# Experts' matrices laid out pair by pair, and one gate piece of each pair loaded for both experts into a tile of twice the size

## The chip, the cores and the metric

The kernel runs on one core of one Trainium2 chip. The metric is device time in microseconds of one execution. The core's five engines are called PE (TensorE, matrix multiplication), DVE (VectorE), ACT (ScalarE), POOL (GpSimd) and SP (SyncE, which here only issues DMAs). A row of the profile's page or of the trace calls them by these names; a DMA issued from SP stands there as SPq.

## The reference

A trunk of two layers over 512 tokens of width 1024, all in float32. A layer is attention in three parallel groups of heads (neighbourhood attention on a grid, latent attention "MLA", windowed attention with a sink) and then a layer of 16 experts in which each expert chooses its tokens:

```python
DEPTH, SEQ, D_MODEL, N_EXPERTS, EC_CAPACITY, D_EXPERT = 2, 512, 1024, 16, 2, 1024
# per layer:
#   h = h + W_out . concat_g( RMSNorm_g( mixer_g(split_g(RMSNorm(h) @ W_in)) ) )
#   h = h + ExpertChoiceSwiGLU(RMSNorm(h))
# ExpertChoiceSwiGLU: each expert takes its SEQ * EC_CAPACITY / N_EXPERTS = 64 best tokens x_e and adds
#   gain * ( (silu(x_e @ w_gate[e]) * (x_e @ w_up[e])) @ w_down[e] )   to their rows
```

Each expert has three matrices of 1024 x 1024 (gate, up, down), 4 MB each, so that a layer's experts are 192 MB, and both layers' 384 MB; every one of these bytes is read once.

## The kernel before, in words

**The expert stage.** Two experts, e and e + 1, make a pair; 64 tokens of each stand side by side on PE. A layer has eight pairs, here called pair 0 to pair 7. The matrices of a pair are read in 24 pieces of 1 MB, each a tile of 128 partitions x 2048 numbers: 8 of gate, 8 of up, 8 of down, always one for e and one for e + 1 behind it. `weights` loads gate pieces (two blocks of 128 rows each), `col_half` up and down pieces; pair 0's first gate pieces are read in halves of 512 KB by `both`. `expert_mm` multiplies; its order is pinned to that of the code. A piece of both experts is 16 matmul instructions on PE (rows call them `in<-ew` or `S<-ew`, line 1163).

**The buffers.** Nearly every large tile of the program, in attention too, comes from one pool, `big`, of 25 buffers of 1 MB (8 KB in each partition): the experts' pieces (`ew`), the input projections' raw matrices (`wraw`), their high and low parts, the up-projection of MLA (`uraw`, split into `uh` and `ul`), the bias tiles of neighbourhood attention (`nab`, 896 KB, one for each of its two pairs of heads and loaded in line 871), the output projection (`woraw`). A tile takes a buffer when the last reader of the tile that had it before is done.

**What sets the order.** The program is written as units that are merged by hand and then put into each engine's order by a scheduler that works before the run; the order of SP's DMAs and the buffer that each tile takes are fixed by it. SP issues its DMAs strictly in that order: one that waits for a buffer holds up all behind it. Each DMA also waits for the DMA eight places ahead of it (eight semaphores, named DMAHW0 to DMAHW7 in the rows of the order), so that eight at most are in flight. The experts' loads of a layer start during its attention, when buffers come free, and then run to the layer's end.

**Names.** "NA pair 2" is the second pair of heads of neighbourhood attention; its scores are the matmuls `S<-nak,naq` (line 856), to which DVE adds the second `nab` tile in line 861. The MLA up-projection multiplies with `uh` and `ul` in lines 161 to 163.

Of the kernel before, what the change touches and what calls it, by code (L numbers as in the profile page):

```python
# [9 lines left out]
F32 = mybir.dt.float32  # L10
# [6 lines left out]
P = 128  # L17
D = 1024
S = 512
NT = S // P  # L20
KD = D // P
DEPTH = 2
NEXP = 16
# [27 lines left out]
C_PERM = C_TRI + 128  # L51
NCST = C_PERM + 512

NB_B = 25
PR = {'SWA': 0, 'NA': 0, 'MLA': 0, 'up': 0}
WARM = [30, 0, 0, 0]
PSB = [2, 1, 1]
# [4 lines left out]
def build(tc, x, w_in, w_uq, w_ukv, w_out, w_gate, w_up, w_down, pv, wr, cst, nab, fin, out):  # L62
    nc = tc.nc
    ctx = ExitStack()
    with ctx:
        const = ctx.enter_context(tc.tile_pool(name="const", bufs=1))
        bpool = ctx.enter_context(tc.tile_pool(name="big", bufs=NB_B))
        spool = ctx.enter_context(tc.tile_pool(name="sm", bufs=1))
        tiny = ctx.enter_context(tc.tile_pool(name="tiny", bufs=2))
        ps = ctx.enter_context(tc.tile_pool(name="ps", bufs=1, space=bass.MemoryType.PSUM))  # L70
# [3 lines left out]
        def nm(s):  # L74
            cnt[0] += 1
            return f"{s}_{cnt[0]}"

        def big(s, dt=F32):
            return bpool.tile([P, 2048], dt, name=nm(s), tag="b")

# [10 lines left out]
        def recut(n):  # L93
            cut[:] = [big("cut", F32R if i == 0 else F32) for i in range(n)]
# [132 lines left out]
        if globals().get("_POOLS") is not None:  # L227
            _POOLS.extend([const, bpool, spool, tiny])

        h = [big("h").rearrange("p (t d) -> p t d", t=NT) for _ in range(2)]  # L230
        c = const.tile([P, NRES], F32, name="c")
        pvt = const.tile([P, DEPTH, NPV], F32, name="pvt")
# [89 lines left out]
        def open_layer(L):  # L322
# [3 lines left out]
            def load(j):  # L326
                raw = big("wraw")[:, :1536].rearrange("p (k n) -> p k n", n=384)
                nc.sync.dma_start(raw, w_in[L, j * 512:(j + 1) * 512, 1184:1568].rearrange("(k p) n -> p k n", p=P))
                w[j] = raw, *(big(n, F32R)[:, :1536].rearrange("p (k n) -> p k n", n=384) for n in ("wh", "wl"))
# [32 lines left out]
        for L in range(DEPTH):  # L362
# [727 lines left out]
            for u in range(NT - 1):  # L1090
                n = NT - 1 - u
# [11 lines left out]
            nc.vector.tensor_tensor(ps2, pcv, ge, op=ALU.mult)  # L1103
            nc.vector.tensor_tensor(pos, ps2[:, :, 0], ps2[:, :, 1], op=ALU.add)

            def weights(w_, e, k0, n):

                ws = []
                for a in range(2):
                    wt = big("ew").rearrange("p (k n) -> p k n", k=n)  # L1110
                    nc.sync.dma_start(wt, w_[L, e + a, k0 // n].rearrange("p (k n) -> p k n", k=n))
                    ws.append(wt)
                return k0, n, ws

            def both(w_, e, k):

                wt = big("ew").rearrange("p (a k n) -> p a k n", a=2, k=1)
                for a in range(2):
                    nc.sync.dma_start(wt[:, a, 0], w_[L, e + a, k // 2, :, k % 2 * D:(k % 2 + 1) * D])
                return k, 1, [wt[:, 0], wt[:, 1]]  # L1120

            def col_half(w_, e, n, ms, cs=slice(0, 512)):

                pieces, k0 = [], 0
                for m in ms:
                    ws = []
                    for a in range(2):
                        wt = big("ew")[:, :m * (cs.stop - cs.start)].rearrange("p (k n) -> p k n", k=m)
                        if cs.stop - cs.start < 512:
                            src = w_[L, e + a, n, cs.start // 256].rearrange("p (k n) -> p k n", k=KD)  # L1130
                            nc.sync.dma_start(wt, src[:, k0:k0 + m])
                        else:
                            src = w_[L, e + a, n, k0 // 4].rearrange("p (k n) -> p k n", k=4)
                            nc.sync.dma_start(wt, src[:, k0 % 4:k0 % 4 + m])
                        ws.append(wt)
                    pieces.append((k0, m, ws))
                    k0 += m
                return pieces

            def up_half(e, n):  # L1140
                return col_half(w_up, e, n, (4, 4))

            def down_half(e, n, ms=(4, 4), cs=slice(0, 512)):
                return col_half(w_down, e, n, ms, cs)

            gate0 = [both(w_gate, 0, k) for k in range(KN["b1"])]
            gate0 += [weights(w_gate, 0, k, 2) for k in range(KN["b1"], KD, 2)]
            up0 = [up_half(0, n) for n in range(2)]
            down0 = [down_half(0, n) for n in range(2)]
# [70 lines left out]
            def hidden(e, gate_w=(), up_w=(), ahead=None, before=None, then=None):  # L1220
# [50 lines left out]
                for i in range(n_gate):  # L1271
                    piece = gate_w[i] if gate_w else weights(w_gate, e, i * 2, 2)
                    k = piece[0] + piece[1]
                    gather_to(k)
                    if done < len(steps):
                        gather_to(k0s[done] + 1)
                    expert_mm(og, xs, piece)
                    if i == i_places:
                        if before:
                            before()  # L1280
                        places()
                    if i == n_gate // 2 and then:
                        then()
# [85 lines left out]
            for e in range(0, NEXP - 2 * tail, 2):  # L1369
                then = None  # L1370
                if e == 4:
                    def then():
                        held.pop(0)()()
                p = hidden(e, gate_w, up0 if e == 0 else (), before=rest, then=then)
                down_w = down0 if e == 0 else [down_half(e, n) for n in range(2)]
                gate_w = [weights(w_gate, 2, k, 2) for k in range(0, KD, 2)] if e == 0 else ()
                if e == 0:
                    held += [half_then(n, down_w[n], *p, held=True) for n in range(2)]
                    continue
                if e == 2:  # L1380
                    token_parts(0)
                rest = half_then(0, down_w[0], *p, held.pop(0)() if e == 4 else None)
                if e == 2:
                    token_parts(1)
                rest = half_then(1, down_w[1], *p, rest)
                if e == 2:
                    st["gather"]()
# [3 lines left out]
            for e in range(NEXP - 2 * tail, NEXP, 2):  # L1391
# [6 lines left out]
                if e < NEXP - 2:  # L1398
                    p = hidden(e, gate_w, (), ahead, rest)
                    gate_w = nxt["gate"]  # L1400
                else:
                    p = hidden(e, gate_w, before=rest)
# [125 lines left out]


def _pairs(w):  # L1530
    return w.reshape(DEPTH, NEXP, 4, 2, P, D).transpose(0, 1, 2, 4, 3, 5).reshape(DEPTH, NEXP, 4, P, 2 * D)


def _halves(w):
    return (w.reshape(DEPTH, NEXP, 2, 4, P, 2, 512).transpose(0, 1, 5, 2, 4, 3, 6)
             .reshape(DEPTH, NEXP, 2, 2, P, 2048))


def _last_quarters(w):

    w = np.array(w)
    v = w[-1, -2:, 1].reshape(2, 2, P, 4, 2, 256)
    w[-1, -2:, 1] = v.transpose(0, 4, 2, 1, 3, 5).reshape(2, 2, P, 2048)
    return w


def _arrays(inp):
    inp = {k: np.asarray(v) for k, v in inp.items()}
    return {
        "x": inp["x"].reshape(S, D),  # L1550
        "w_in": inp["w_in"],
        "w_uq": inp["mla_w_uq"],
        "w_ukv": inp["mla_w_ukv"],
        "w_out": inp["w_out"],

        "w_gate": _pairs(inp["w_gate"]),
        "w_up": _halves(inp["w_up"]),
        "w_down": _last_quarters(_halves(inp["w_down"])),
        "pv": _pack(inp),
        "wr": inp["w_router"].reshape(DEPTH, KD, P, NEXP).transpose(0, 2, 1, 3).reshape(DEPTH, P, NWR),  # L1560
        "cst": _constants(),
        "nab": _na_bias(inp["na_rpb"]),
        "fin": np.ascontiguousarray(np.broadcast_to(inp["final_norm"][None], (P, D))),
    }
# [17 lines left out]
```

## Time and profile before

| | |
|---|---|
| three timed runs | 1532.13, 1536.1, 1537.83 us; median 1536.1 |
| profiled execution | 1538.31 us, of which the span of the trace is 1535.2 us |
| clock granted to PE, mean | 0.985 |
| PE busy | 1454.9 us (95% of the span) |
| DMA | 444.98 MB, mean 290 GB/s over the span |

The time of the profiled execution holds 3.1 us that lie outside the span; it is 2.2 us above the median of the timed runs. All times below count from the span's start. In layer 0 the attention goes on to about 305 us and the experts to about 752; in layer 1 the attention ends at about 1072 and the experts at about 1520.

### The profile page before, as it was taken

What the parts mean: (1) busy time and instruction counts of PE and PEld (TensorE: products, weight loads), DVE (VectorE), ACT (ScalarE), POOL (GpSimd) and SP (SyncE); (2) the same over time, 40 slices, a digit from 0 to 9 for tenths busy, and PEclk for the clock granted to TensorE, in tenths of its full rate; (3) what the DMA queues carried; (4) which work ended last, traced back from release to release, by engine and by line L of the source; (5) the groups of instructions that cost most, each with busy time, mean ns of one, the idle gap of its engine ahead of it and who ended that gap; (6) DMA issues with size and microseconds to landing.
All of it is one profiled execution on the core that took longest, in us unless ns stands there. A gap on an engine that the chain in (4) does not pass through costs nothing.

```text
span 1535.2 us, 21197 instructions
## 1 busy us (share of the span) xinstructions
PE 1454.9 (95%) x8262; PEld 861.9 (56%) x8262; DVE 597.6 (39%) x1513; ACT 364.7 (24%) x939; POOL 241.0 (16%) x341
## 2 busy tenths in 40 slices
PE   9999999899999999987999998898999999999886
PEld 8987877544444434432489876675444344344323
DVE  6766675710222212110376587557102222121113
ACT  4434645300200000001134355442001000000012
POOL 3532442000200000000133335320002000000002
PEclk9999999999999999999999999999999999999998
DMA  5122263789999999999711214447899999999996
GB/s 201 51 71 78 83 190 142 310 332 397 390 415 421 421 420 421 421 421 418 304 55 53 69 51 141 132 157 306 329 397 394 415 421 421 421 421 421 421 421 243
DMA packets 80434, 444.98 MB, mean 290 GB/s; under 512 B 7760, under 2 KB 23632, under 8 KB 32464
## 3 DMA queue, kind: packets, MB, share of 16 engines
q1 hardware_dynamic: 76688, 438.40, 71.5%
q0 software_dynamic: 3648, 5.24, 1.7%
q8 instruction: 65, 1.06, 0.3%
q14 instruction: 33, 0.27, 0.1%
HBM read 436.28 MB, written 2.10 MB: 286 GB/s over the span
## 4 chain that ended last, share of the span: by engine, by line
PE 78%; DMA 14%; DVE 4%; ACT 2%; issue 1%; POOL 1%; DVEq 0%; SPq 0%; ACTq 0%; POOLq 0%
PE S L1163 20%; PE in L1163 15%; PE in L161 5%; DMA ew<-in_w_up_dram 5%; PE in L163 5%; PE in L162 5%; PE tr L155 4%; PE o L297 4%; DMA ew<-in_w_down_dram 4%; DMA ew<-in_w_gate_dram 4%; PE tr L1213 3%; PE tr L1200 2%; PE tr L1341 2%; PE trq L1341 1%; DMA mq<-mq 1%; PE trq L998 1%
## 5 line engine op out<-in xcount | busy, mean ns | idle before, releaser
L1163 PE MATMUL S<-ew,PT 128*64 128x512 f32 x960 | 214.0, 595 | 2.4 <-DMA ew<-in_w_down_dram 2.4
L1163 PE MATMUL S<-ew,xs 128*64 128x512 f32 x768 | 173.6, 594 | 11.8 <-DMA ew<-in_w_up_dram 11.8
L1163 PE MATMUL in<-ew,xs 128*64 128x512 f32 x768 | 172.6, 595 | 5.6 <-DMA ew<-in_w_gate_dram 5.6
L1163 PEld LDWEIGHTS S<-ew,PT 128*64 128x64 f32 x960 | 67.0, 137 | 133.2 <-issue 127.3
L1298 DVE SCALAR_TENSOR_TENSOR sb<-S,rsl,sb 128x512 f32<-128x512 f32 x32 | 24.0, 751 | 302.5 <-PE S L1163 302.5
L1163 PEld LDWEIGHTS S<-ew,xs 128*64 128x64 f32 x768 | 57.3, 137 | 126.1 <-issue 98.7
L1163 PEld LDWEIGHTS in<-ew,xs 128*64 128x64 f32 x768 | 54.4, 137 | 109.0 <-issue 97.3
L146 POOL TENSOR_SCALAR wh<-wraw 128x384 fp32r<-128x384 f32 (+2 forms) x40 | 35.9, 919 | 367.7 <-DMA ew<-in_w_down_dram 300.0
L161 PE MATMUL in<-wh,hT 128*128 128x256 f32 (+1 forms) x256 | 77.5, 304 | 0.0
L163 PE MATMUL in<-wh,hT 128*128 128x256 f32 (+1 forms) x256 | 77.4, 303 | 0.0
L162 PE MATMUL in<-wl,hT 128*128 128x256 f32 (+1 forms) x256 | 77.2, 302 | 0.0
L1287 ACT ACTIVATE sb<-in,rsl 128x512 f32<-128x512 f32 x32 | 21.4, 686 | 228.2 <-PE in L1163 181.0
L1163 PE MATMUL in<-ew,PT 128*64 128x512 f32 (+1 forms) x352 | 73.9, 559 | 0.0
L1342 DVE TENSOR_TENSOR h<-h,trq 128x512 f32<-128x512 f32 (+1 forms) x31 | 20.8, 671 | 131.6 <-PE trq L1341 131.6
L146 POOL TENSOR_SCALAR sb<-sb,cut 128x512 f32<-128x512 f32 (+2 forms) x64 | 46.1, 721 | 103.3 <-DVE cut L569 66.7
L155 PE MATMUL tr<-c,sb 128*128 128x128 f32 x324 | 55.0, 285 | 6.2 <-DVE sb L1298 4.2
L1322 ACT ACTIVATE PT<-tr 128x512 f32<-128x512 f32 x24 | 14.3, 597 | 185.5 <-PE tr L155 185.5
L1448 POOL TENSOR_TENSOR fo<-h,fg 128x512 f32<-128x512 f32 x4 | 5.0, 1279 | 338.0 <-DMA fg<-in_fin_dram 338.0
L146 POOL TENSOR_SCALAR cut<-cut,cut 128x512 f32<-128x512 f32 (+2 forms) x64 | 44.9, 702 | 77.1 <-DVE cut L569 57.2
L152 POOL TENSOR_TENSOR hl<-h,hh 128x512 fp32r<-128x512 f32 x16 | 19.9, 1275 | 214.0 <-ACT hh L1178 214.0
L149 DVE SCALAR_TENSOR_TENSOR sb<-S,asl,sb 128x512 fp32r<-128x512 f32 x18 | 13.5, 752 | 102.2 <-ACT sb L143 102.2
L155 PEld LDWEIGHTS tr<-c,sb 128*128 128x128 f32 x324 | 36.6, 145 | 26.3 <-issue 14.4
(386 smaller groups left out, 2799.3 us busy)
## 6 DMA issues: line engine op xcount, KB each, us to landing
ew<-in_w_up_dram SPq DMA_DIRECT2D x128, 1024.0 KB, 16.9
ew<-in_w_down_dram SPq DMA_DIRECT2D x124, 1024.0 KB, 17.7
ew<-in_w_gate_dram SPq DMA_DIRECT2D x120, 1024.0 KB, 17.6
wraw<-in_w_in_dram SPq DMA_DIRECT2D x8, 1024.0 KB, 8.9
ew<-in_w_gate_dram SPq DMA_DIRECT2D x16, 512.0 KB, 8.1
woraw<-in_w_out_dram SPq DMA_DIRECT2D x6, 1024.0 KB, 5.0
nab<-in_nab_dram SPq DMA_DIRECT2D x4, 896.0 KB, 5.5
wraw<-in_w_in_dram SPq DMA_DIRECT2D x4, 832.0 KB, 4.8
```

What stands on the lines that cost most here:

```text
L146: nc.gpsimd.tensor_scalar(o, i, r, 1.0, op0=ALU.mult, op1=ALU.mult)
L155: return nc.tensor.transpose(o, i, ident)
L161: nc.tensor.matmul(o, lh, rh, start=start, stop=False)
L162: nc.tensor.matmul(o, lh, rl, start=False, stop=False)
L163: nc.tensor.matmul(o, ll, rh, start=False, stop=stop)
L297: nc.tensor.matmul(o[a * 64:(a + 1) * 64, :], v_of(a, kb), PTs[a][:, i * P:(i + 1) * P], start=(i == 0), stop=(i == len(kbs) - 1))
L1163: pinned(nc.tensor.matmul(o[n][a * 64:(a + 1) * 64, :], src[k // 4][:, k % 4, a * 64:(a + 1) * 64], ws[a][:, k - k0, n * 512:n * 512 + o[n ...
L1200: pinned(nc.tensor.matmul(pg[:, k], h[k0 // 4][:, t, (k0 % 4 + k) * P:(k0 % 4 + k + 1) * P], oh[:, t], start=(t == 0), stop=(t == NT - 1)))
L1213: pinned(nc.tensor.matmul(pg[:, k], x[k0 // 4][:, t, cs], oh[:, t], start=(t == 0 and x is st["parts"][0]), stop=(t == NT - 1 and x is st[ ...
L1287: nc.scalar.activation(s, og[n], AF.Silu, scale=rsl)
L1298: nc.vector.scalar_tensor_tensor(sg[j], ou, rsl, sg[j], op0=ALU.mult, op1=ALU.mult)
L1341: pinned(nc.tensor.matmul(o, G[:, t * P:(t + 1) * P], y[j], start=(j == 0), stop=(j == 1)))
```

## The change

The pool `big` has 23 buffers in place of 25, and a new pool, `double`, has one tile of 2 MB (16 KB in each partition). The experts' matrices are stored in HBM pair by pair: for each piece and each partition, 8 KB of expert e and behind them 8 KB of expert e + 1. An ordinary load of 1 MB so reads rows of 8 KB that stand 16 KB apart; before, its rows stood directly one behind the other. One gate piece of each pair (the first; in pair 0 the third of its four) is loaded for both experts with one DMA of 2 MB into the new tile. The matmuls and their order within the experts' code stay as they are; 16 loads fewer are issued (8 in each layer).

```diff
-NB_B = 25
+NB_B = 23
+
+NB_D = 1
...
         bpool = ctx.enter_context(tc.tile_pool(name="big", bufs=NB_B))
+        dpool = ctx.enter_context(tc.tile_pool(name="double", bufs=NB_D))
...
+        def double(s):
+            return dpool.tile([P, 2, 2048], F32, name=nm(s), tag="d")
...
+            def in_one(w_piece, k):
+
+                wt = double("ed")
+                nc.sync.dma_start(wt, w_piece)
+                return [wt[:, a].rearrange("p (k n) -> p k n", k=k) for a in range(2)]
+
             def weights(w_, e, k0, n):
 
+                if k0 == (0 if e else 4):
+                    return k0, n, in_one(w_[L, e // 2, k0 // n], n)
                 ws = []
                 for a in range(2):
                     wt = big("ew").rearrange("p (k n) -> p k n", k=n)
-                    nc.sync.dma_start(wt, w_[L, e + a, k0 // n].rearrange("p (k n) -> p k n", k=n))
+                    nc.sync.dma_start(wt, w_[L, e // 2, k0 // n, :, a].rearrange("p (k n) -> p k n", k=n))
                     ws.append(wt)
                 return k0, n, ws
...
 def _pairs(w):
-    return w.reshape(DEPTH, NEXP, 4, 2, P, D).transpose(0, 1, 2, 4, 3, 5).reshape(DEPTH, NEXP, 4, P, 2 * D)
+    return (w.reshape(DEPTH, NEXP // 2, 2, 4, 2, P, D).transpose(0, 1, 3, 5, 2, 4, 6)
+             .reshape(DEPTH, NEXP // 2, 4, P, 2, 2 * D))
```

The same change of index, from expert to pair and half, stands in `both`, `col_half`, `_halves` and `_last_quarters`.

The pools change the order that the scheduler finds. Three places of it matter below. In the rows, `waits` names the semaphores that the instruction waits for; the name ahead of the arrow is the tile written, behind it what is read.

**First place: SP in layer 0, the end of pair 4's loads and the start of pair 5's.** Before, the down pieces of pair 4 are followed by the eight gate pieces of pair 5 (line 1111):

```order
L1134 DMA ew_4588<-in_w_down_dram 128x2048 [waits DMAHW4_49,PE_49]
L1134 DMA ew_4590<-in_w_down_dram 128x2048 [waits DMAHW5_49,PE_49]
L1111 DMA ew_4655<-in_w_gate_dram 128x2048 [waits DMAHW6_49,PE_49]
L1111 DMA ew_4657<-in_w_gate_dram 128x2048 [waits DMAHW7_49,PE_49]
L1111 DMA ew_4667<-in_w_gate_dram 128x2048 [waits DMAHW0_49,PE_49]
L1111 DMA ew_4669<-in_w_gate_dram 128x2048 [waits DMAHW1_49,PE_49]
L1111 DMA ew_4709<-in_w_gate_dram 128x2048 [waits DMAHW2_49,PE_49]
```

In the changed kernel, whose lines are 1115 for the double tile (`ed`), 1125 for the other gate pieces and 1148 for up and down, the same stretch reads:

```order
L1115 DMA ed_4648<-in_w_gate_dram 128x4096 [waits DMAHW3_49,PE_49]
L1148 DMA ew_4573<-in_w_down_dram 128x2048 [waits DMAHW4_49,PE_49]
L1148 DMA ew_4575<-in_w_down_dram 128x2048 [waits DMAHW5_49,PE_49]
L1148 DMA ew_4577<-in_w_down_dram 128x2048 [waits DMAHW6_49,PE_49]
L1148 DMA ew_4579<-in_w_down_dram 128x2048 [waits DMAHW7_49,PE_49]
L1148 DMA ew_4581<-in_w_down_dram 128x2048 [waits DMAHW0_49,PE_49]
L1148 DMA ew_4583<-in_w_down_dram 128x2048 [waits DMAHW1_49,PE_49]
L1125 DMA ew_4658<-in_w_gate_dram 128x2048 [waits DMAHW2_49,PE_49]
L1125 DMA ew_4660<-in_w_gate_dram 128x2048 [waits DMAHW3_49,PE_49]
L1115 DMA ed_4793<-in_w_gate_dram 128x4096 [waits DMAHW4_49,PE_49]
L1125 DMA ew_4700<-in_w_gate_dram 128x2048 [waits DMAHW5_49]
L1125 DMA ew_4702<-in_w_gate_dram 128x2048 [waits DMAHW6_49]
```

`ed_4648` is pair 5's double piece and now stands ahead of pair 4's last six down pieces; `ed_4793` is pair 6's, and stands ahead of pair 5's third and fourth gate pieces (`ew_4700` and those behind it) and of all its up pieces. There is one double tile, so that the PE value for which `ed_4793` waits is that of the last matmul on `ed_4648`, the end of pair 5's first gate piece. The loads behind it wait for no value of PE of their own. The same order stands at the same place in layer 1.

**Second place: SP in layer 0, the loads of pair 7, the last.** Before, down pieces follow one another behind a load for the next layer's projection (`wraw`):

```order
L1134 DMA ew_5213<-in_w_up_dram 128x2048 [waits DMAHW5_49,PE_49]
L328 DMA wraw_5246<-in_w_in_dram 128x4x384 [waits DMAHW6_49,PE_49]
L1134 DMA ew_5250<-in_w_down_dram 128x2048 [waits DMAHW7_49,PE_49]
L1134 DMA ew_5252<-in_w_down_dram 128x2048 [waits DMAHW0_49,PE_49]
L1134 DMA ew_5254<-in_w_down_dram 128x2048 [waits DMAHW1_49,PE_49]
L1134 DMA ew_5256<-in_w_down_dram 128x2048 [waits DMAHW2_49,PE_49]
```

In the changed kernel:

```order
L1148 DMA ew_5200<-in_w_up_dram 128x2048 [waits DMAHW5_49,PE_49]
L334 DMA wraw_5233<-in_w_in_dram 128x4x384 [waits DMAHW6_49,PE_49]
L1148 DMA ew_5237<-in_w_down_dram 128x2048 [waits DMAHW7_49,PE_49]
L1148 DMA ew_5239<-in_w_down_dram 128x2048 [waits DMAHW0_49,PE_49]
L1148 DMA ew_5241<-in_w_down_dram 128x2048 [waits DMAHW1_49,PE_49]
L1115 DMA ed_8552<-in_w_gate_dram 128x4096 [waits DMAHW2_49,PE_49]
L1148 DMA ew_5243<-in_w_down_dram 128x2048 [waits DMAHW3_49,PE_49]
```

`ed_8552` is the double piece of pair 0 of layer 1: 2 MB for the next layer stand ahead of the fourth of pair 7's first four down pieces.

**Third place: PE in layer 0's attention, around the MLA up-projection and the scores of NA pair 2.** Before, the scores that take the second bias tile (`S_2110`, `S_2122`, line 856) stand between the up-projection's matmuls (`ul`, line 162), of which ten are still to come:

```order
L161 MATMUL in_2041<-uh_1707,MR_328 128x288
L162 MATMUL in_2041<-ul_1708,MR_328 128x288
L163 MATMUL in_2041<-uh_1707,cut_209 128x288
L855 MATMUL S_2110<-nak_1537,naq_1467 128x384
L856 MATMUL S_2110<-nak_1537,naq_1468 128x384
L158 MATMUL tr_1991<-ident_r,un_1750 128x128
```

In the changed kernel (lines 167 to 169 for the up-projection, 861 and 862 for the scores) the same scores come after the last matmul on `ul`:

```order
L167 MATMUL in_2205<-uh_1710,MR_331 128x384
L168 MATMUL in_2205<-ul_1711,MR_331 128x384
L169 MATMUL in_2205<-uh_1710,cut_212 128x384
L164 MATMUL trq_2219<-ident_r,un_1753 128x128
L164 MATMUL trq_2239<-ident_r,un_1753 128x128
L164 MATMUL trq_2239<-ident_r,kn_2191 128x128
L164 MATMUL trq_2239<-ident_r,un_1753 128x128
L861 MATMUL S_2113<-nak_1540,naq_1470 128x384
L862 MATMUL S_2113<-nak_1540,naq_1471 128x384
```

With 23 buffers the second `nab` tile takes the buffer of `ul`; its load waits for the value of PE that this last matmul sets, and SP's later loads of the attention stand behind it. Before, it took the buffer of a tile that was done earlier. Layer 1 has the same buffer for it and the same wait.

## Rows read from the trace of the kernel before

**Rows 1.** Table by stretch: busy us by engine, clock, DMA share, GB/s.

```profile
core 0: us, PE busy (x) PEld busy (x) DVE busy (x) ACT busy (x) POOL busy (x), PEclk, DMA share, GB/s
...
100.00:200.00 100.00, 94.35 (x628) 79.33 (x626) 69.85 (x202) 53.68 (x162) 40.20 (x63) 0.97 0.29 85
...
400.00:500.00 100.00, 99.64 (x494) 44.10 (x492) 27.01 (x52) 11.83 (x20) 9.98 (x8) 1.00 1.01 419
...
640.00:730.00 90.00, 77.24 (x340) 27.00 (x337) 8.32 (x15) 7.79 (x11) 1.94 (x4) 1.00 1.01 420
...
1365.00:1490.00 125.00, 113.13 (x546) 47.09 (x542) 16.22 (x33) 10.14 (x15) 0.00 (x0) 1.00 1.01 421
```

**Rows 2.** PE's timeline at the end of layer 0's experts: start, length, idle before.

```profile
720.89 3.22 PE L1163 MATMUL S<-ew,PT 128*64 128x512 f32 x13 [1.31 <-DMA ew<-in_w_down_dram]
...
725.86 3.65 PE L1163 MATMUL in<-ew,hk 128*64 128x512 f32 x14 [1.32 <-DMA ew<-in_w_down_dram]
```

**Rows 3.** The chain that ended last, near layer 1's end: start, length.

```profile
1470.45 19.80 DMA ew<-in_w_down_dram
1490.29 3.65 PE in L1163 x14
```

**Rows 4.** SP's timelines, pair 5's gate loads, layer 0 and layer 1.

```profile
550.73 17.85 SPq L1111 DMA_DIRECT2D ew<-in_w_gate_dram  x8
...
1317.51 17.62 SPq L1111 DMA_DIRECT2D ew<-in_w_gate_dram  x8
```

**Rows 5.** DMA issues, 550:600 and 1310:1365: KB each, median us to landing.

```profile
ew<-in_w_gate_dram SPq DMA_DIRECT2D x8, 1024.0 KB, 20.2
...
ew<-in_w_gate_dram SPq DMA_DIRECT2D x8, 1024.0 KB, 19.8
```

**Rows 6.** PE's timelines, the start of pair 5, layer 0 and layer 1.

```profile
580.91 7.04 PE L1163 MATMUL in<-ew,xs 128*64 128x512 f32 x32
...
591.09 7.09 PE L1163 MATMUL in<-ew,xs 128*64 128x512 f32 x32
...
1347.43 7.04 PE L1163 MATMUL in<-ew,xs 128*64 128x512 f32 x32
```

**Rows 7.** DMA issues into an empty queue, 238.9:239.3, and the page's list.

```profile
ew<-in_w_gate_dram SPq DMA_DIRECT2D x1, 1024.0 KB, 4.9
...
woraw<-in_w_out_dram SPq DMA_DIRECT2D x6, 1024.0 KB, 5.0
```

**Rows 8.** The tile nab, layer 0 and then layer 1.

```profile
L861 DVE CUSTOM_DVE_ANT_0 sb<-S,nab x8: 409/482/558, 151.7 to 194.2; 128x256 f32<-128x256 f32 x4, 128x384 f32<-128x384 f32 x4
L871 SPq DMA_DIRECT2D nab<-in_nab_dram x2: 328/334/340, 123.2 to 164.2; - x2
DMA to landing us min/median/max: 4.9/5.1/5.3
...
L861 DVE CUSTOM_DVE_ANT_0 sb<-S,nab x8: 408/482/558, 908.9 to 955.0; 128x256 f32<-128x256 f32 x4, 128x384 f32<-128x384 f32 x4
L871 SPq DMA_DIRECT2D nab<-in_nab_dram x2: 327/348/369, 879.4 to 922.0; - x2
```

**Rows 9.** The tile ul: layer 0, layer 1; then DVE's first use of the second nab.

```profile
L162 PE MATMUL in<-ul,MR x24: 290/297/442, 156.1 to 193.1; 128*128 128x288 f32 x16, 128*128 128x384 f32 x8
...
L162 PE MATMUL in<-ul,MR x24: 292/296/442, 913.6 to 952.2; 128*128 128x288 f32 x16, 128*128 128x384 f32 x8
...
177.27 0.41 DVE L861 CUSTOM_DVE_ANT_0 sb<-S,nab 128x256 f32<-128x256 f32 x1
```

**Rows 10.** The program's start: SP's second wraw load, POOL's split, PE's use.

```profile
4.54 0.46 SPq L328 DMA_DIRECT2D wraw<-in_w_in_dram  x1
...
14.18 1.94 POOL L146 TENSOR_SCALAR wh<-wraw 128x384 fp32r<-128x384 f32 x4 [2.58 <-DMA wraw<-in_w_in_dram]
...
20.08 0.41 PE L161 MATMUL trq<-wh,hT 128*128 128x384 f32 x1 [0.43 <-ACT hT L143]
```

More of the change, by code (lines that the diff above doesn't have):

```diff
@@ L1118, in both @@
                 for a in range(2):
-                    nc.sync.dma_start(wt[:, a, 0], w_[L, e + a, k // 2, :, k % 2 * D:(k % 2 + 1) * D])
+                    nc.sync.dma_start(wt[:, a, 0], w_[L, e // 2, k // 2, :, a, k % 2 * D:(k % 2 + 1) * D])
                 return k, 1, [wt[:, 0], wt[:, 1]]
@@ L1129, in col_half @@
                         if cs.stop - cs.start < 512:
-                            src = w_[L, e + a, n, cs.start // 256].rearrange("p (k n) -> p k n", k=KD)
+                            src = w_[L, e // 2, n, cs.start // 256, :, a].rearrange("p (k n) -> p k n", k=KD)
                             nc.sync.dma_start(wt, src[:, k0:k0 + m])
                         else:
-                            src = w_[L, e + a, n, k0 // 4].rearrange("p (k n) -> p k n", k=4)
+                            src = w_[L, e // 2, n, k0 // 4, :, a].rearrange("p (k n) -> p k n", k=4)
                             nc.sync.dma_start(wt, src[:, k0 % 4:k0 % 4 + m])
@@ L1530, in _pairs @@
 def _pairs(w):
-    return w.reshape(DEPTH, NEXP, 4, 2, P, D).transpose(0, 1, 2, 4, 3, 5).reshape(DEPTH, NEXP, 4, P, 2 * D)
+    return (w.reshape(DEPTH, NEXP // 2, 2, 4, 2, P, D).transpose(0, 1, 3, 5, 2, 4, 6)
+             .reshape(DEPTH, NEXP // 2, 4, P, 2, 2 * D))
 def _halves(w):
-    return (w.reshape(DEPTH, NEXP, 2, 4, P, 2, 512).transpose(0, 1, 5, 2, 4, 3, 6)
-             .reshape(DEPTH, NEXP, 2, 2, P, 2048))
+    return (w.reshape(DEPTH, NEXP // 2, 2, 2, 4, P, 2, 512).transpose(0, 1, 6, 3, 5, 2, 4, 7)
+             .reshape(DEPTH, NEXP // 2, 2, 2, P, 2, 2048))
 def _last_quarters(w):
     w = np.array(w)
-    v = w[-1, -2:, 1].reshape(2, 2, P, 4, 2, 256)
-    w[-1, -2:, 1] = v.transpose(0, 4, 2, 1, 3, 5).reshape(2, 2, P, 2048)
+    v = w[-1, -1, 1].reshape(2, P, 2, 4, 2, 256)
+    w[-1, -1, 1] = v.transpose(4, 1, 2, 0, 3, 5).reshape(2, P, 2, 2048)
     return w
```

## The prediction

> **What bounds the kernel now.** I read the table by stretch first. In attention PE is busy 94 us of 100 and the DMA engines 29% of the time. In the first part of a layer's experts PE is still busy 99.6 us of 100, while the DMA engines are already at 1.01 and 419 GB/s: PE eats what was loaded ahead. Later, 640 to 730 us, PE falls to 77 of 90 at the same DMA rate, and in layer 1 to 113 of 125 [rows 1]. PE's timeline says why: a piece of both experts takes PE 3.65 us, and PE then stands 1.3 us until the next has landed, still so at 720.89 and 725.86, the last down pieces of layer 0 [rows 2]. The chain that ended last has the same in layer 1: a down load from 1470.45 to 1490.25, then PE [rows 3]. So from there to the end of either expert stage the loads set the time, and a microsecond for which the DMA engines stand idle earlier in the saturated stretch, or are given another layer's bytes, is a microsecond at the end of that stage. SP's timeline gives the rate: eight loads of 1 MB are issued in 17.85 us, one every 2.5 us (17.62 and 2.48 in layer 1) [rows 4], and each lands about 20 us after its issue [rows 5], which is eight times 2.5. Attention is bound by PE, so what is late there counts when PE has nothing else to do.
>
> **Bytes and capacity.** The same bytes are read at the same places in the chip; 25 MB are at hand for pieces before and after (23 of 1 MB, one of 2). Neither moves a sum. What moves is who waits for which buffer.
>
> **Pair 5's bubble, both layers.** The load of pair 6's double piece waits for the end of pair 5's first gate piece and stands ahead of pair 5's third and fourth gate pieces and its up pieces. SP holds all of them. Only pair 5's first two gate pieces, four 1-MB shares, are issued before. Priced by the times of before: the gate loads began at 550.73 [rows 4], so the fourth share was issued at 550.73 + 3 x 2.5 = 558.3 and landed 20.2 later [rows 5], at 578.5. PE starts pair 5 at 580.91, with two pieces in 7.04 us [rows 6], so the first is done at 584.4. Only then does the next load go, into an empty queue, where the first 1 MB lands after 4.9 us [rows 7]: 589.3. Before, the fifth share landed at 581.0. The stream is 8.3 us later. Layer 1: the fourth share lands at 1317.51 + 3 x 2.48 + 19.8 = 1344.8, the fifth at 1347.2; PE's first piece ends at 1347.43 + 3.5 = 1350.9, the next MB lands at 1355.8: 8.6 us later. In the place itself PE needs the third piece at 591.09 [rows 6], and it comes behind the 2 MB of pair 6, at 589.3 + 2.5 + 5.0 = 596.8: a stall of 5.7 us at once, part of the 8.3 and not beside it, because pair 6 finds its first piece there. The rest appears where the loads set the time. Together **+17**. Bounds: a queue that isn't quite empty, so that one cold load alone shows, 4.9 for each layer (10); the stall of 5.7 not given back, 14 for each (28). I take 17, the nearest to the rows.
>
> **The next layer's double piece in layer 0's tail.** 2 MB for layer 1 stand ahead of the fourth of pair 7's first four down pieces, where PE waits for each load as it lands [rows 2]. Two shares of 2.5 us: **+5.0**. Bounds: 3.7, if 1.3 of it falls into a wait that another engine ends, and 5.0. Layer 1 gets nothing back: its first pieces are loaded in attention, where the DMA engines are idle 71% of the time [rows 1].
>
> **The second bias tile, both layers.** Before, it was issued at 164.2 and took 5.1 us, so it was there at 169.3 [rows 8]; DVE first used it at 177.27 [rows 9], 8 us later. Now its load waits for the last matmul on `ul`, which before was at 193.1 [rows 9], about when NA pair 2 was through (last use 194.2, [rows 8]). So this pair's eight softmax pieces can no longer lie between the up-projection's matmuls; PE takes the up-projection to its end first, as the third place of the order shows, and then has the bias load before it. Low bound for a layer: the bare load, 5.1, with PE filled till then and after. High bound: the whole stretch of its use, 177.3 to 194.2, comes behind everything else of that part, 17. PE has MLA's scores and the output projection as other work, but those need DVE and ACT, which are 70% and 54% busy here [rows 1]. I take 10, between them, nearer to the load: PE is not left without any work. Layer 1 has the same order (issue 922.0, last use 955.0, [rows 8]; last `ul` matmul 952.2, [rows 9]): 10. Together **+20**, 10 to 34.
>
> **Edits at nothing.** The double piece of pair 0 goes at the very start ahead of the second `wraw` load, issued at 4.54; that lands 5 us later. Its split on POOL began at 14.18, and PE uses it from 20.08 [rows 10]: 5.9 us of cover against 5.0. Without that cover it costs up to 5. Sixteen loads fewer on SP: a DMA takes SP 0.4 to 0.5 us [rows 10] against 2.5 us of the DMA engines for each MB, so SP isn't what is short. The 16-KB pitch of the ordinary loads: rows of 8 KB as before, no row of before shows the pitch; from the 421 GB/s [rows 1] I take no loss (rival 3).
>
> [...]
>
> **Sum.** 17 + 5 + 20 = +42 on the span of 1535.2: 1577; with the 3.1 us outside it 1580 for that execution, which was 2.2 above the median. Against the median of 1536.1: **1578 us**.
>
> **The rivals.**
> 1. *The bias tile is hidden.* PE fills the wait with the up-projection and MLA's scores, and nothing is late behind it. For it: DVE isn't the bound. Against: DMA, bias and softmax stand one behind the other. Then +22: 1558.
> 2. *The bubble is hidden,* if the pieces loaded ahead last to the end of the stage. Against: PE waits for each load at 720 us [rows 2]. Then 25: 1561.
> 3. *The pitch slows the loads.* Saturated stretches are about 350 us in each layer (400 to 750, and as long in layer 1): each per cent costs 7 us in all. For it: nothing in the trace. At 5%: 1578 + 35 = 1613.
> 4. *Faster: a 2-MB load saves one load's fixed part.* A lone 1-MB load lands after 4.9 us [rows 7], of which 2.5 are its share of the rate, so that 2.4 are fixed; 16 loads fewer give 39, if the fixed part shows in each: 1536 - 39 = 1497, if nothing of the above shows beside it (with the +42 it would be 1539). It decides from the point where loads land more than 2.5 us apart with eight in flight. Against: they are issued at just 2.5, and 421 GB/s is what a full queue gives.
> 5. *No change:* all three waits fall into slack.
>
> The rule behind the fourth is in the Trainium skill, "DMA: Bandwidth & Descriptors", Anatomy of one DMA: a fixed 2.0 us and bytes over 436 GB/s. By it two loads of 1 MB take 8.8 us and one of 2 MB 6.8, so 16 would save an estimated 32 us; the trace's loads overlap, so it doesn't add here.
>
> **How the numbers follow.** Half a per cent, 7.7 us, is about what a measurement of this kernel can tell from no change. The forecast with all three waits, +24 to +56, has 0.65; rival 1 0.12, rival 2 0.06, rival 3 0.10, rival 4 0.03, rival 5 0.04. The low bounds (10 + 3.7 + 10 = 24: 1560) and rival 1 (1558) set the lower end, with 3 us for the spread of the runs: 1555. The upper end takes the high bound of the bias tile with the rest as it stands (34 + 17 + 5 = 56): 1592, and 2 for the spread: 1594. Left out are rival 3 above 2%, and 4 and 5: some 0.17. Faster 0.03, same 0.04, slower 0.93.
>
> **What would show it.** In the changed trace: (a) at pair 5 of each layer the DMA engines idle for some 8 us (DMA share under 1 in a stretch that was full), SP waiting for PE at the double piece, PE waiting some 5.7 us for gate; (b) in layer 0's tail one wait of about 6.3 us in place of 1.3; (c) the second bias tile issued after the last `ul` matmul, DVE's first use of it 5 us later, and attention longer by 5 to 17 us in each layer; (d) 1 MB every 2.5 us elsewhere. The prediction is wrong if the saturated rate differs from 421 GB/s by more than 2%, if attention ends when it did, or if the DMA engines stay full at pair 5.

## The result, and the profile of the changed kernel

| | before | changed |
|---|---|---|
| median of four runs, us | 1536.96 | 1574.56 |
| lowest and highest, us | 1532.13 and 1540.98 | 1571.89 and 1582.08 |
| ratio, with its 95% interval | | 1.0253 [1.0229, 1.0276] |

The changed kernel is 38 us slower (forecast: 42, 1578). The execution that was profiled is the slowest of the four, 1582.08 us with a span of 1579.9 and a mean granted clock of 0.967, where the other three have 0.977 to 0.982. What the attention of this one execution adds is read with that in mind.

The place at pair 5 of layer 0, in the table by stretch (columns as in [rows 1]):

```profile
580.00:590.00 10.00, 9.66 (x50) 3.48 (x47) 0.75 (x1) 1.19 (x2) 0.00 (x0) 1.00 1.02 424
590.00:600.00 10.00, 10.00 (x46) 3.92 (x44) 3.23 (x5) 1.24 (x2) 0.00 (x0) 1.00 0.51 211
600.00:610.00 10.00, 9.47 (x50) 4.66 (x46) 3.76 (x9) 0.13 (x1) 0.00 (x0) 1.00 0.62 233
610.00:620.00 10.00, 6.07 (x14) 1.58 (x16) 1.79 (x5) 0.00 (x0) 0.00 (x0) 0.66 1.01 425
```

The DMA engines go from full to half and back: 5.0 + 3.9 us of them idle. SP's waits in 575:610 and its timeline there (start, length) say what it stood for:

```profile
SPq L1115 <- PE in L1177: 20.8, 1, 20.8
```

```profile
574.66 5.25 SPq L1125 DMA_DIRECT2D ew<-in_w_gate_dram  x2
602.87 0.33 SPq L1115 DMA_DIRECT2D ed<-in_w_gate_dram  x1
603.25 2.47 SPq L1125 DMA_DIRECT2D ew<-in_w_gate_dram  x4
```

SP stands 20.8 us at pair 6's double load (line 1115), until PE (line 1177 is `expert_mm`) is through with pair 5's; then five loads go within 2.9 us, into an empty queue. Layer 1 has the same, by SP's waits in 1360:1395:

```profile
SPq L1115 <- PE in L1177: 20.7, 1, 20.7
```

PE's timeline shows both ends of it, and, further on, the tail of the layer:

```profile
599.23 3.60 PE L1177 MATMUL in<-ed,xs 128*64 128x512 f32 x16
602.66 3.60 PE L1177 MATMUL in<-ew,xs 128*64 128x512 f32 x16
...
613.42 1.97 PE L1177 MATMUL in<-ew,xs 128*64 128x512 f32 x2 [3.96 <-DMA ew<-in_w_gate_dram]
615.90 8.49 PE L1177 MATMUL in<-ew,xs 128*64 128x512 f32 x29 [0.51 <-DMA ew<-in_w_gate_dram]
...
742.97 3.65 PE L1177 MATMUL S<-ew,PT 128*64 128x512 f32 x16 [0.79 <-DMA ew<-in_w_down_dram]
752.84 4.86 PE L1177 MATMUL S<-ew,PT 128*64 128x512 f32 x13 [6.22 <-DMA ew<-in_w_down_dram]
```

A wait of 6.22 us stands where [rows 2] had 1.31, at the fourth of pair 7's first four down pieces: the 2 MB of the next layer went ahead of it. In the tile `nab` of layer 0 (as [rows 8]) and in `ul` (as [rows 9]) the second bias tile is issued after the last matmul on `ul`, and DVE waits for it:

```profile
L867 DVE CUSTOM_DVE_ANT_0 sb<-S,nab x8: 417/489/558, 153.5 to 211.1; 128x256 f32<-128x256 f32 x4, 128x384 f32<-128x384 f32 x4
L877 SPq DMA_DIRECT2D nab<-in_nab_dram x2: 328/334/341, 130.5 to 195.7; - x2
  DMA nab<-in_nab_dram: 2.5, 1
```

```profile
L168 PE MATMUL in<-ul,MR x24: 292/337/525, 160.3 to 195.3; 128*128 128x288 f32 x16, 128*128 128x384 f32 x8
```

Its issue moves from 164.2 to 195.7, 0.4 us after the last of those matmuls began, and its last use from 194.2 to 211.1.

To compare kernels I cut each profiled execution at four marks that PE's timeline shows: the first gather of each layer's experts (`tr<-qn,h`), the short wait (0.8 us) at the third of pair 7's first-half down pieces in layer 0 and the next wait behind it, and in layer 1 the wait that answers to [rows 3], which is the last one for a load except in pools23 and bub_k6. Those two have one more behind it, by which the layer ends some 1.2 and 1.5 us later than their last column tells. For the changed kernel the marks of layer 0's tail are the rows at 742.97 and 752.84, and that of layer 1 is:

```profile
1535.43 3.65 PE L1177 MATMUL in<-ew,hk 128*64 128x512 f32 x14 [1.31 <-DMA ew<-in_w_down_dram]
```

| us between marks | attention 0 | experts 0 | tail | attention 1 | experts 1 |
|---|---|---|---|---|---|
| before | 307.5 | 408.4 | 5.0 | 353.1 | 416.3 |
| changed | 325.8 | 417.1 | 9.9 | 357.6 | 425.0 |
| layout | 307.5 | 409.5 | 5.0 | 349.5 | 416.3 |
| pinned | 316.0 | 413.3 | 5.0 | 358.5 | 420.8 |
| pinned_nab | 305.2 | 413.2 | 5.0 | 351.0 | 421.0 |
| pin_ends | 315.6 | 417.1 | 5.0 | 357.6 | 424.8 |
| bubbles | 306.6 | 416.9 | 5.0 | 352.1 | 425.0 |
| bub_no6 | 306.5 | 408.5 | 5.0 | 347.6 | 417.2 |
| bias_only | 317.2 | 408.9 | 5.0 | 354.5 | 416.3 |
| pools23 | 317.6 | 414.5 | 5.0 | 359.0 | 421.2 |
| bub_k6 | 305.6 | 415.5 | 5.0 | 347.1 | 423.3 |
| best | 307.7 | 408.5 | 5.0 | 353.2 | 416.4 |

The rows below the second are the experiments that follow. Where nothing in the experts was changed that costs, their columns repeat to about 1 us from kernel to kernel; attention 1 repeats only to some 6.

### The profile page after: what moved, and what is told of

It is laid out like the page before. It is cut to its first block, busy times and chain, and to the rows that moved or that the text cites. A ratio compares the mean times of both kernels' runs of the same rounds, so it can differ in the third digit from the quotient of the medians.

```text
span 1579.9 us, 21150 instructions
## 1 busy us (share of the span) xinstructions
PE 1478.8 (94%) x8262; PEld 872.7 (55%) x8262; DVE 600.4 (38%) x1513; ACT 367.4 (23%) x939; POOL 241.4 (15%) x341
## 4 chain that ended last, share of the span: by engine, by line
PE 70%; DMA 21%; DVE 4%; ACT 2%; issue 1%; POOL 1%; SPq 0%; DVEq 0%; ACTq 0%; POOLq 0%
PE S L1177 18%; PE in L1177 12%; DMA ew<-in_w_up_dram 7%; DMA ew<-in_w_gate_dram 6%; PE in L167 5%; PE in L169 5%; PE in L168 5%; PE tr L161 4%; PE o L303 4%; DMA ew<-in_w_down_dram 4%; PE tr L1227 2%; PE tr L1214 2%; DMA wraw<-in_w_in_dram 1%; PE tr L1355 1%; DMA ed<-in_w_gate_dram 1%
## 5 line engine op out<-in xcount | busy, mean ns | idle before, releaser
L1177 PE MATMUL in<-ew,xs 128*64 128x512 f32 x576 | 138.7, 613 | 9.9 <-DMA ew<-in_w_gate_dram 9.9
L1177 PEld LDWEIGHTS in<-ew,xs 128*64 128x64 f32 x576 | 42.1, 141 | 93.8 <-issue 76.6
L1356 DVE TENSOR_TENSOR h<-h,trq 128x512 f32<-128x512 f32 (+1 forms) x31 | 20.8, 671 | 126.1 <-PE trq L1355 126.1
L1177 PE MATMUL in<-ew,PT 128*64 128x512 f32 (+1 forms) x288 | 60.1, 551 | 0.0
## 6 DMA issues: line engine op xcount, KB each, us to landing
ew<-in_w_up_dram SPq DMA_DIRECT2D x128, 1024.0 KB, 18.3
```

The source lines that it names most:

```text
L1177: pinned(nc.tensor.matmul(o[n][a * 64:(a + 1) * 64, :], src[k // 4][:, k % 4, a * 64:(a + 1) * 64], ws[a][:, k - k0, n * 512:n * 512 + o[n ...
L1356: nc.vector.tensor_tensor(h[n][:, t, cs], h[n][:, t, cs], o, op=ALU.add)
```

## The experiments

Each is given with its median, beside the kernel before of the same chip job, and the ratio to it with its 95% interval.

**layout: only the layout.** 25 buffers, no double piece, pair by pair.

```diff
-NB_B = 23
+NB_B = 25
...
-                if k0 == (0 if e else 4):
+                if False:
```

> The matrices pair by pair with rows 16 KB apart, but 25 buffers and no double piece. My theory (the order of the loads and the bias tile cost, the layout nothing): 1537, within 4 us of the kernel before, saturated stretches at 420 to 421 GB/s. Rival (the pitch slows the loads): 7 us for each per cent of rate; if it made the whole difference, 1575 and about 400 GB/s in the saturated stretches.

Measured 1537.64 against 1537.35, 1.0007 [0.9988, 1.0025]. The saturated stretches run as in [rows 1]:

```profile
400.00:500.00 100.00, 99.64 (x494) 44.10 (x492) 27.01 (x52) 11.79 (x20) 9.97 (x8) 1.00 1.01 418
...
1365.00:1490.00 125.00, 113.01 (x546) 46.33 (x543) 16.70 (x33) 9.68 (x14) 0.00 (x0) 1.00 1.01 421
```

Rows of 8 KB at a pitch of 16 KB cost nothing here. The rival falls.

**pin_ends: pair 0's and pair 7's loads in the order of the code.** `first_or_last` keeps an instruction in program order for e = 0 and e = 14 alone; it stands around the experts' other loads in the same way.

```diff
-                nc.sync.dma_start(wt, w_piece)
+                first_or_last(e, nc.sync.dma_start(wt, w_piece))
```

> The changed kernel with only pair 0's and pair 7's loads kept in the order of the code: the double piece of pair 0 is loaded neither at the program's start nor in layer 0's tail; the bubbles at pair 5 and the bias tile's wait stay. My theory: 5 from the tail and 3 to 4 from the start come off: 1565 to 1567. Rival (what the tail loads early is given back in layer 1, and the start is hidden): 1573 to 1575.

Measured 1569.15, 1.0211 [1.0187, 1.0235]: 31.8 above before, where the changed kernel is 37.6 above, so 5.8 less. The tail column falls from 9.9 to 5.0 and layer 1's columns don't change, so nothing is seen to be given back there. That leaves about 0.9 for the start by the medians, which agree with anything from nothing to some 4, since the runs of the changed kernel lie 10 us apart. The profiles say more. In the first 100 us, of the changed kernel and then of this one, PE is 2.8 us busier without the early load:

```profile
0.00:100.00 100.00, 93.80 (x652) 86.09 (x653) 66.11 (x154) 39.81 (x110) 44.04 (x60) 0.98 0.40 130
```

```profile
0.00:100.00 100.00, 96.58 (x679) 87.92 (x680) 65.11 (x156) 40.40 (x111) 42.99 (x61) 1.00 0.36 118
```

In the changed kernel POOL's split of the second `wraw` tile begins at 20.65, where [rows 10] had 14.18:

```profile
20.65 2.55 POOL L152 TENSOR_SCALAR wh<-wraw 128x384 fp32r<-128x384 f32 x4 [8.89 <-DMA wraw<-in_w_in_dram]
```

Further on PE comes to the same matmul 3.95 us later than here (PE's timeline, the changed kernel first):

```profile
104.88 0.46 PE L164 MATMUL trq<-ident_r,qn 128*128 128x128 f32 x4
```

```profile
100.93 0.46 PE L164 MATMUL trq<-ident_r,qn 128*128 128x128 f32 x4
```

In each of the other ten kernels of the table that matmul starts between 100.5 and 101.0. So the early load put PE some 4 us back in the first 100 us of the profiled execution; what of it is left in the median, the runs don't settle.

**bubbles: pin_ends with the second bias tile in the double tile,** which is empty in attention. In each kernel that has it there, its load is kept in the order of the code as well.

```diff
-                                st["bias"] = big("nab")[:, :1792].rearrange("p (h n) -> p h n", h=2)
+                                st["bias"] = (double("nab")[:, 1] if pair else big("nab"))[:, :1792].rearrange("p (h n) -> p h n", h=2)
```

> Double piece of pair 0 in the order of the code (no tail, no early start) and the second bias tile in the double tile: only the bubbles at pair 5 are left. My theory: 8.7 us for each layer's experts, as in the profile of the changed kernel, so 1537 + 17 = 1554, and attention as in the kernel before. Rival (the expert stages lose by something else, as the 4.8 us for each layer that the kernel with all loads in the order of the code still lost): 1547.

Measured 1550.96 against 1536.42, 1.0097 [1.0075, 1.0119]. The expert columns are those of the changed kernel, 8.5 and 8.7 above before, and attention is that of before.

**bub_no6: the same, but pair 6's piece in two ordinary loads.**

```diff
-                if k0 == (0 if e else 4):
+                if e != 12 and k0 == (0 if e else 4):
```

> As the one with only the bubbles left, but pair 6's first gate piece is loaded with two ordinary loads, so that no load waits for pair 5's double piece ahead of pair 5's own loads. My theory: the bubbles go, 1537 to 1541 (up to 4 for the double tile that stands empty from pair 5 to pair 7). Rival (the bubble is not what the pair 6 piece causes): 1554, as the one with the bubbles.

Measured 1534.76, 0.9986 [0.9972, 1.0000]. One load less of the double kind in each layer takes off 16.2 us, and at pair 5 the DMA engines stay full (table by stretch):

```profile
570.00:580.00 10.00, 10.00 (x48) 4.00 (x46) 3.23 (x5) 0.69 (x1) 0.00 (x0) 1.00 1.01 420
580.00:590.00 10.00, 10.00 (x54) 4.85 (x50) 3.09 (x5) 0.69 (x1) 0.00 (x0) 1.00 1.01 422
590.00:600.00 10.00, 10.00 (x48) 3.38 (x49) 2.46 (x9) 1.38 (x2) 0.00 (x0) 1.00 1.02 423
```

The expert columns are 0.1 and 0.9 above before: seven other double loads in each layer cost next to nothing, so neither 2 MB in one DMA nor a single tile costs by itself.

**bias_only: bub_no6 with the bias tile back in the pool of 23.**

> No bubble at pair 5 (pair 6 has two ordinary loads), no tail, no early start; the second bias tile takes the buffer of ul again and waits for the up-projection. My theory, that the parts add up: 1535 for the same kernel with the bias tile in the double tile, and 18 to 19.5 for the bias tile, 1553 to 1555, all of it in the two attentions (the first experts' gather some 9 to 11 us later in layer 0, attention of layer 1 some 6 to 8 us longer). Rival (the bias tile's lateness only showed together with the blocked loads): 1535 to 1541.

Measured 1552.03 against 1537.11, 1.0102 [1.0081, 1.0123]; 16.6 above bub_no6, each against the kernel before of its own job. Attention 0 is 10.7 longer than there, attention 1 6.9. PE's waits in 150:240 (us in total, times, longest) show where the first of it goes:

```profile
PE S L861 <- DVE cut L867: 2.9, 1, 2.9
PE trq L164 <- DVE un L158: 2.7, 2, 1.8
PE in L167 <- ACT MF L149: 1.9, 2, 1.1
```

All of PE's waits in this stretch sum to 11.2 us, and in bub_no6 to 4.1, with none above 1.1; so 7.1 of the 10.7 are PE standing. The granted clock over attention 0 is 0.97 here and 0.98 there, which would make some 3 us (0.01 of 317), an estimate to the rounding of these figures.

**pinned and pinned_nab: all of the experts' loads in the order of the code,** the second with the bias tile in the double tile as well.

```diff
-                nc.sync.dma_start(wt, w_piece)
+                tc.keep_in_program_order(nc.sync.dma_start(wt, w_piece))
```

> The changed kernel with the experts' loads kept in the order of the code, so that each double piece is issued just ahead of its own pair's other gate pieces; double tile, 23 buffers and the bias tile's wait stay. My theory: the two bubbles (17), the tail (5) and the start (3 to 4) go, the bias tile's part of attention stays: 1547 to 1553, DMA share at or above 1.00 at pair 5. Rival (a 2 MB load, or a single buffer for it, costs by itself): 1570 to 1575, as the changed kernel.

> As the one with the order of the code, and besides the second bias tile of each layer lies in the double tile, which is empty in attention, so that its load doesn't wait for the MLA up-projection. My theory: 1536 to 1541, the rest of attention as before. Rival (with 23 buffers other loads and tiles of attention are late, not the bias tile): 1547 to 1553, no better than the one with the order of the code alone.

Measured 1560.05, 1.0150 [1.0126, 1.0173], and 1540.59, 1.0024 [1.0010, 1.0039]. Between the two the bias tile makes 19.5 us, 10.8 and 7.5 by the attention columns. But pinned is 7 us above what I expected, and the expert columns of both are 4.5 to 4.9 above before. I first took that for 2 MB less loaded ahead, two shares of 2.48 us; the next kernel was to show it.

**pools23: 23 buffers, no double tile.**

> 23 buffers, no double tile, ordinary loads, layout pair by pair. Attention has the bias tile's wait for the up-projection: 18 to 20 us in both layers together. The expert stages: if the 4.8 us for each layer that the kernel with all loads in the order of the code lost are 2 MB less of pieces loaded ahead (two shares of 2.48 us), they stand here too: 1565. If they belong to the double tile itself, they don't: 1556.

Measured 1564.21 against 1536.42, 1.0185 [1.0158, 1.0213]. The expert columns are 6.1 and 4.9 above before. By the expectation that speaks for fewer pieces loaded ahead; but this kernel would lose by them in any case, having 23 MB for pieces in place of 25, and pinned may lose by something else as much. It was no test of that. The trace of pinned settles it. Its table by stretch, just after the experts of layer 0 start, and SP's waits in 318:345:

```profile
316.00:326.00 10.00, 10.00 (x66) 6.72 (x68) 2.42 (x8) 0.00 (x0) 0.00 (x0) 1.00 0.66 251
326.00:336.00 10.00, 10.00 (x62) 5.22 (x60) 2.42 (x8) 0.00 (x0) 0.00 (x0) 1.00 0.01 2
336.00:346.00 10.00, 10.00 (x50) 3.41 (x48) 0.00 (x0) 2.55 (x3) 0.00 (x0) 1.00 0.88 349
```

```profile
SPq L1115 <- PE in L1177: 15.9, 1, 15.9
```

The order of the code has a bubble of its own, at pair 1: its double load stands ahead of all its other gate loads and waits for PE to be done with pair 0's piece. 10 us of idle DMA engines cost 4.9, because the kernel before isn't always busy here either: its share is 0.72 in the same stretch, and it idles a little later, for want of buffers, where this one doesn't:

```profile
317.50:327.50 10.00, 10.00 (x60) 5.20 (x58) 2.45 (x8) 0.00 (x0) 0.00 (x0) 1.00 0.72 253
...
377.50:387.50 10.00, 10.00 (x54) 3.98 (x52) 1.13 (x4) 1.26 (x2) 0.00 (x0) 1.00 0.68 274
387.50:397.50 10.00, 10.00 (x48) 3.16 (x44) 0.75 (x1) 0.00 (x0) 0.00 (x0) 1.00 0.92 359
```

What counts is the sum. In the 140 us from the first gather on, the kernel before, pinned and pools23 move:

```profile
307.50:447.50 140.00, 139.26 (x740) 65.17 (x742) 24.25 (x54) 15.11 (x24) 9.98 (x8) 1.00 0.94 380
```

```profile
316.00:456.00 140.00, 139.26 (x740) 65.15 (x742) 24.23 (x54) 15.11 (x24) 9.98 (x8) 1.00 0.89 365
```

```profile
317.60:457.60 140.00, 139.27 (x740) 65.24 (x742) 24.23 (x54) 15.11 (x24) 9.98 (x8) 1.00 0.95 380
```

Pinned is 2.1 MB behind by then, 5.0 us at 420 GB/s, and its column is 4.9 above before; in layer 1 it has 366 against 380 GB/s, 4.7 us, and its column is 4.5 above. Pools23 isn't behind, so its own loss has another cause; that it is the fewer pieces loaded ahead is argued, not shown.

**bub_k6: the last gate piece of each pair is the double one.**

```diff
-                if k0 == (0 if e else 4):
+                if k0 == 6:
```

> As the one with only the bubbles left, but the last gate piece of each pair is the double one in place of the first; in the order that this gives, each double piece stands ahead of its own pair's other gate pieces and never ahead of the pair before's. My theory: a 2 MB load costs nothing by itself, the position of the wait does: 1537 to 1542. Rival (one double tile for eight pairs costs wherever the piece lies): 1550 to 1555.

Measured 1544.66 against 1536.42, 1.0058 [1.0040, 1.0075]: neither number. Again the trace has a bubble, in another place. SP's timeline, and the table by stretch:

```profile
454.91 14.64 SPq L1154 DMA_DIRECT2D ew<-in_w_up_dram  x8
491.49 0.33 SPq L1121 DMA_DIRECT2D ed<-in_w_gate_dram  x1
491.87 4.15 SPq L1154 DMA_DIRECT2D ew<-in_w_down_dram  x7
```

```profile
485.00:495.00 10.00, 10.00 (x50) 3.31 (x46) 1.74 (x5) 1.37 (x2) 0.00 (x0) 1.00 0.29 93
```

The load of the next pair's piece waits 21.9 us by SP's waits, with seven down loads behind it that were free to go. They are the pair before's, so what I expected of the order was wrong too. The expert columns lose 7.1 and 7.0, together more than the 8.2 of the whole: attention is 7.9 shorter in this execution than before (bub_no6 has it 6.5 shorter), and no run says why. So a 2 MB load costs next to nothing (bub_no6), but one tile for it does wherever its wait stands ahead of other loads for long enough to run the queue dry.

**best: bub_no6 with both bias tiles in the two halves of the double tile.**

> No bubble, no tail, no early start, and both bias tiles of a layer lie in the double tile's two halves, so that neither takes one of the 23 buffers in attention. My theory: attention has one buffer more than in the kernel with only the second one there, the rest is the same: 1531 to 1536. Rival (buffers are no longer what attention waits for): no different from that kernel's 1535; in no case above 1538.

Measured 1536.65 against 1537.11, 0.9998 [0.9985, 1.0011]. Neither this nor bub_no6 beats the kernel before by what can be told. It also speaks against a rival for the bias tile's price, that the buffer counts which it leaves free and not its wait: a second one left free brings nothing.

## Why the prediction was right, point by point

**Pair 5's bubble** was forecast at 8.3 and 8.6 us; the expert columns rise by 8.7 and 8.7, and taking away the one load that waits takes off 16.2 in all. The stall on the spot was forecast at 5.7. PE's rows show 3.96 + 0.51 of idle time, and between the two only two matmuls, in 1.97 us: `expert_mm` takes the two experts in turn, so the piece goes on only when the second expert's 1 MB is there, at 615.90. PE had been free from 609.46 (613.42 less the 3.96), 6.4 us before. Less the two matmuls that is some 6, near the forecast. The rest shows later.

**The next layer's piece in the tail**: 5.0 forecast, 4.9 measured, the wait 6.22 where 6.3 was named; not seen to be given back in layer 1. One reading was wrong without effect: the rows at 720.89 and 725.86 are not the last down pieces of layer 0 but the last for which PE waits; it multiplies with more of them afterwards and finds them landed.

**The second bias tile**: 10 forecast for each layer, between 5 and 17; the pairs of kernels that differ in it alone give 10.7 and 10.8 in layer 0, 6.9 and 7.5 in layer 1, and 16.6 and 19.5 in the whole. Layer 1's is 2.5 to 3 below the forecast, in a column that repeats to some 6 us, so the runs can't say that it pays less. The sign that was named, 5 to 17 us in each layer, is missed on both sides by the changed kernel's own profile, 18.3 in layer 0 and 4.5 in layer 1; the first has more in it than the bias tile, as the sum below tells.

**Start, pitch, fewer loads**: forecast at nothing. The pitch is shown to cost nothing. The start was forecast as covered with 0.9 us to spare, and it wasn't: the split began 6.5 us late in place of 5, and in the profiled execution PE was 4 us behind at 101 us. By the medians between nothing and 4 us of it is left. Sixteen loads fewer save nothing that can be seen (bub_no6, with 14 fewer, is even with before).

**The sum.** By the experiments 16.6 (bias) + 16.2 (bubbles) + 5.8 (tail and start) = 38.6 from bub_no6, which is 1.7 below before: 36.9, against 37.6 measured. The terms add up to within the few us that each is known to. The forecast of 42 is high mostly by what it gave the bias tile; what the start cost beyond its nothing makes up for a part of that, by luck. In the profiled execution attention 0 is 18.3 longer than before; 8.1 of that is in pin_ends too. Of the other 10.2, 4 are the start's, and from 200 us on the granted clock is 0.92 against 0.97 there, which makes some 6, an estimate (0.05 of 126 us): this execution is 7.5 us above its kernel's median.

The rivals: the bias tile isn't hidden (bias_only), the bubble isn't (bubbles), the pitch doesn't slow the loads (layout), and a larger load gives nothing back (bub_no6), as the rows with loads 2.5 us apart had said. The rule of the Trainium skill that the prediction names beside this last one ("DMA: Bandwidth & Descriptors", Anatomy of one DMA) is fitted to single DMAs issued from GpSimd; here SP issues them, eight in flight.

## What to carry to other kernels

Before giving one kind of load a buffer of its own, look at where its wait will stand in the queue that issues in order: with a single buffer, each of these loads waits for the consumer of the one before, and every load behind it waits too, though its own buffer is free. Here SP issued nothing from 579.9 to 602.87, 23 us, with eight loads in flight; 14 of them were hidden and 8.9 were not. Taking buffers out of a shared pool has a second price in stages that look unrelated: see which tile inherits whose buffer, and when that one's last reader is done.

## What the runs showed of the hardware that was not expected

PE's granted clock fell after stretches with gaps. In the changed kernel's first attention, by the table by stretch, PE was busy 8.58 of 10 us at the full clock; in the next 10 the granted clock was 0.64, and in the 10 after them PE stood for 4.1:

```profile
170.00:180.00 10.00, 8.58 (x68) 6.27 (x67) 3.48 (x13) 4.78 (x14) 1.58 (x3) 1.00 0.10 15
180.00:190.00 10.00, 8.59 (x48) 7.80 (x48) 5.39 (x15) 5.45 (x16) 1.79 (x3) 0.64 0.00 0
190.00:200.00 10.00, 5.92 (x30) 4.72 (x29) 3.90 (x10) 4.42 (x11) 1.78 (x3) 0.84 0.32 107
200.00:210.00 10.00, 8.50 (x45) 6.57 (x45) 5.98 (x23) 6.18 (x18) 5.50 (x9) 0.67 0.40 123
```

A granted clock of 1.00 is 2.4 GHz throughout; 0.64 is 7.2 of the 10 us at 1.2 GHz. The stall at pair 5 has the same behind it: 0.66 in 610:620, where the three stretches before it have 1.00. In a stage that PE bounds, a stall could so cost more than its own length. How much of the bias tile's price it is, no run separates; the 3 us estimated for bias_only are the nearest.
